# Where four blocks of modulation weights run: amid the attention, or among and behind the projections

## The chip, the core and the metric

The kernel runs on one NeuronCore of a Trainium2 chip. The metric is the time of the whole program on the device in microseconds (us). The five engines are named as in the profile: PE (matmul; PEld is its weight load), DVE (vector), ACT (scalar), POOL (GpSimd) and SP (which here only issues transfers). All of them run their own instruction lists in order and meet at semaphores.

## What is computed

One step of a one-layer decoder for a prompt group (512 tokens) and a sample group (8 sequences of 4 tokens) that share the weights. Both are modulated by six vectors that come from a conditioning vector c by one matrix of 1024 x 6144, in 12 blocks of 512 columns:

```python
def layer(x, c, ...):
    m = silu(c) @ w_ada + b_ada          # 6 modulation vectors of 1024
    sh1, sc1, g1, sh2, sc2, g2 = split(m, 6)
    h = rmsnorm(x) * (1 + sc1) + sh1
    u = h @ w_in                         # q, k, v of three branches, gates, z, xBC, dt
    o_nsa = nsa(u)                       # compressed, selected and window attention
    y_ssm = mamba2(u)                    # conv, scan, gate
    x = x + g1 * (concat(norm(o_nsa), norm(y_ssm)) @ w_out)
    h2 = rmsnorm(x) * (1 + sc2) + sh2
    return x + g2 * moe(h2)              # 16 experts, 2 per token
```

For the sample group the keys of 2048 earlier tokens are read from paged caches. The compressed branch takes pooled rows of a cache (a weighted sum over 32 rows), the selected branch gathers 16 blocks that the compressed scores choose.

## The kernel before

The program has three stages. In the **projections** the product with `w_in` runs in the pieces C, z, q and B, with three matmuls for each product (a weight split into `wh` and `wl`, the input into `hH` and `hL`, tile `acc`). Between the pieces stand the steps of the prompt's scan (p, c0 to c3, e). The string `ORDER` sets the sequence; `f1` in it calls `fill`, which runs one filler, and the table `BETWEEN` puts further fillers inside the pieces. A filler is either a pooling batch (`pool_batch`: two gathers of 1 MB of the compressed cache, issued by POOL, then 64 matmuls with `gcmp` and `PW`) or a modulation block (`ada_block`: two loads of 1 MB, `wada`, issued by SP, then 64 matmuls with the transposed conditioning vector `scT`, 8 with the bias `bada`, and one copy by ACT into `mods`). `in_turn` chains the matmuls of successive fillers so that PE takes them in that order. All these weights, gathers and the `w_in` pieces share a pool of 7 slots of 1 MB (`SLOT`, `load_w`), which is handed round in program order: a load starts when the reader of the slot's former content is through.

In the **attention**, `attend(t, b)` works through the prompt's branches (`s<-KT,QT`, softmax on DVE and ACT, transposes `pt<-ident,psb`, then `ot`), while the sample's chain (`sel_first`, `sel_second`: gathers `gsel`, tiles `sm`, `smo`; and the sample's scan, `sbm`, `xcS`, `s2k`) is a row of dependent steps. Then come the **output projection** and the **experts**.

Blocks 0 to 3 of the modulation are computed at the start. Blocks 4 to 7 are fillers. Blocks 8 to 11 (`sc2` and `g2`) run, before the change, amid the attention, just ahead of `attend(3, 1, True)`: `late_rows` loads their 8 MB through two buffers named `wt`, and their matmuls are summed in the tile `pt`, of which there are two buffers that `attend` also uses for its transposes. `store_mods` writes `mods` to DRAM (`modd`), from where the output projection loads it in other layouts (`M`, `MS`, `h2T`).

Of the kernel before, what the change touches and what calls it, by code (L numbers as in the profile page):

```python
# [9 lines left out]
F32 = mybir.dt.float32  # L10
# [7 lines left out]
P = 128  # L18
# [4 lines left out]
TS = 4  # L23
NS = NB * TS
NE = 16
ORDER = "C p z c0 c1 q c2 f1 f1 c3 e B"
WB = 6
XAT = 4
LA = 4
# [21 lines left out]
def hybrid_step(ctx: ExitStack, tc: tile.TileContext, a, o):  # L51
    nc = tc.nc
    V, S, G, T, SP = nc.vector, nc.scalar, nc.gpsimd, nc.tensor, nc.sync
# [19 lines left out]
    def W(pl, shape, dt, tag, bufs=2):  # L73
        return pl.tile(list(shape), dt, name=nm(tag), tag=tag, bufs=bufs)
# [85 lines left out]
    w_ada = a["w_ada"][0].rearrange("(k p) n -> p k n", p=P)  # L160
# [18 lines left out]
    p1, close_p1 = pool("p1")  # L179
# [125 lines left out]
    def store_mods(n0, n1):  # L305
        for j in range(4):
            SP.dma_start(modd[:, n0:n1, j, :], mods[32 * j:32 * j + 9, n0:n1, :])
# [52 lines left out]
    def in_turn(f, *args):  # L360

        traced = nc.cur_bb.bb.instructions
        n0 = len(traced)
        r = f(*args)
        for i in traced[n0:]:
            if i.engine == mybir.EngineType.PE:
                if tail[0] is not None:
                    tc.add_manual_dep(i, tail[0].name, mybir.DependencyInfo(mybir.DependencyClass.NoSync,
                                                                            mybir.DependencyReason.DATA),
                                      reason="in_turn")  # L370
                tail[0] = i
        return r
# [157 lines left out]
    for kv, w8 in enumerate((wk8, wv8)):  # L530
# [4 lines left out]
    V.tensor_scalar_mul(Wp[:, 1], Wp[:, 0], wkp[:, 1:2])  # L535
    V.tensor_scalar_mul(Wp[:, 0], Wp[:, 0], wkp[:, 0:1])

    fillers = [(pool_batch if c == "p" else ada_block, int(i)) for c, i in
               (f for f in "p0 a4 p1 a5 p2 p3 a6 p4 p5 a7 p6 p7".split())]

    def fill(n=1):
        for _ in range(n):
# [4 lines left out]
                   B={1: (fill,), 3: (fill,), 5: (fill,)})  # L547
# [287 lines left out]
    for step in ORDER.split():  # L835
# [3 lines left out]
            ssd_chunk(int(step[1:]))  # L839
        else:  # L840
            steps[step]()
    store_mods(0, 4)
    close_ph()
    close_p1()
    close_psum()
# [520 lines left out]
    attend(2, 1, True)  # L1366
    sel_second(1, gt11, *first1)

    def late_rows(n):
        ts = []  # L1370
        for hf in range(2):
            t = W(p3, [P, 2, 4, 256], F32, "wt", 2).rearrange("p b i c -> p (b i c)").rearrange("p (k c) -> p k c", k=4)
            SP.dma_start(t, w_ada[:, 4 * hf:4 * hf + 4, n * 512:n * 512 + 512])
            ts.append(t)
        return lambda k: ts[k // 4][:, k % 4, :]

    for n in range(8, 12):
        in_turn(ada_block, n, late_rows(n), "pt")
    store_mods(4, 8)
    attend(3, 1, True)  # L1380

    k3 = kcv[:, 0:P].rearrange("p (g d) -> p g d", d=64)
# [805 lines left out]
```

## Time and profile before

| | us |
|---|---|
| program, median of 3 runs | 811.96 (806.91 to 815.54) |
| program, the profiled execution | 813.91 |
| its span | 812.2 |
| PE busy in the span | 714.6 (88%) |
| DVE busy | 492.2 (61%) |
| ACT busy | 348.4 (43%) |
| POOL busy | 142.1 (17%) |

The span is what the profiler saw of the engines; 1.7 us of the program's time lie outside of it. Times in the rows are us from the start of the span. A granted clock of 1.00 is TensorE at 2.4 GHz, and 0.5 would be 1.2 GHz. Busy times overlap between engines.

### The profile page before, as it was taken

What the parts mean: (1) busy time and instruction counts of PE and PEld (TensorE: products, weight loads), DVE (VectorE), ACT (ScalarE), POOL (GpSimd) and SP (SyncE); (2) the same over time, 40 slices, a digit from 0 to 9 for tenths busy, and PEclk for the clock granted to TensorE, in tenths of its full rate; (3) what the DMA queues carried; (4) which work ended last, traced back from release to release, by engine and by line L of the source; (5) the groups of instructions that cost most, each with busy time, mean ns of one, the idle gap of its engine ahead of it and who ended that gap; (6) DMA issues with size and microseconds to landing.
All of it is one profiled execution on the core that took longest, in us unless ns stands there. A gap on an engine that the chain in (4) does not pass through costs nothing. (4 is left out here: it accounts for less than half of the span.)

```text
span 812.2 us, 14470 instructions
## 1 busy us (share of the span) xinstructions
PE 714.6 (88%) x5484; PEld 519.0 (64%) x5484; DVE 492.2 (61%) x1302; ACT 348.4 (43%) x799; POOL 142.1 (17%) x165
## 2 busy tenths in 40 slices
PE   4999999899897999659989788899948999999993
PEld 3677877777674766437456365678835676667662
DVE  7443783526529774354324644758996797887773
ACT  3324444425234435311133344623433575677671
POOL 3012021231313101012000100003131222224221
PEclk9999999899996979865599899999859999999997
DMA  8954885054474661482635310748858899998311
GB/s 287 391 128 154 297 307 205 2 189 151 180 272 164 233 232 46 163 311 104 196 122 206 112 45 1 235 156 285 323 175 339 247 311 338 316 335 281 85 22 26
DMA packets 67259, 161.86 MB, mean 199 GB/s; under 512 B 19171, under 2 KB 31404, under 8 KB 60788
## 3 DMA queue, kind: packets, MB, share of 16 engines
q1 hardware_dynamic: 56964, 115.54, 40.8%
q0 software_dynamic: 10224, 45.37, 16.6%
q8 instruction: 44, 0.72, 0.4%
q14 instruction: 27, 0.22, 0.1%
HBM read 153.48 MB, written 20.74 MB: 215 GB/s over the span
## 5 line engine op out<-in xcount | busy, mean ns | idle before, releaser
L892 ACT ACTIVATE psb<-s,amx 128x128 f32<-128x128 f32 (+3 forms) x64 | 33.2, 523 | 53.4 <-DVE amx L888 26.2
L95 PE MATMUL acc<-wh,hH 128*128 128x512 f32 (+1 forms) x128 | 49.2, 385 | 0.5 <-PE acc L95 0.5
L95 PE MATMUL acc<-wl,hH 128*128 128x512 f32 (+1 forms) x128 | 47.6, 372 | 0.0
L95 PE MATMUL acc<-wh,hL 128*128 128x512 f32 (+1 forms) x128 | 47.4, 370 | 0.0
L95 PE MATMUL acc<-gu,XF 128*128 128x512 f32 x88 | 46.5, 611 | 0.0
L95 PE MATMUL acc<-wh,XH 128*128 128x512 f32 x68 | 44.5, 655 | 0.4 <-ACT XH L1954 0.4
L344 DVE TENSOR_TENSOR wl<-dn,wh 128x512 fp32r<-128x512 f32 x52 | 34.1, 686 | 8.3 <-ACT wh L343 8.2
L895 PE MATMUL pt<-ident,psb 128*128 128x128 f32 x160 | 30.3, 298 | 10.0 <-ACT psb L892 9.4
L105 ACT COPY kt<-sm 128x512 f32<-128x512 f32 x33 | 19.0, 586 | 41.6 <-PE sm L1036 31.1
L344 DVE TENSOR_TENSOR wl<-gu,wh 128x512 fp32r<-128x512 f32 x44 | 29.6, 688 | 10.4 <-ACT wh L343 8.8
L343 ACT CAST wh<-dn 128x512 fp32r<-128x512 f32 x52 | 30.8, 619 | 10.7 <-PE acc L95 8.8
L2003 POOL DMA_INDIRECT out_y_prompt<-yo,gi x13 | 21.2, 1629 | 76.7 <-DVE gi L1923 16.8
L95 PE MATMUL acc<-wh,HH 128*128 128x512 f32 x68 | 32.3, 478 | 2.1 <-ACT HH L1986 2.1
L1071 POOL DMA_INDIRECT gsel<-in_cache_sel,idx x16 | 16.0, 1001 | 100.2 <-PE smo L95 71.2
L343 ACT CAST wh<-gu 128x512 fp32r<-128x512 f32 x44 | 26.2, 619 | 16.7 <-PE acc L95 10.3
L895 PEld LDWEIGHTS pt<-ident,psb 128*128 128x128 f32 x160 | 18.9, 150 | 19.0 <-ACT psb L892 14.8
L1724 POOL TENSOR_TENSOR h<-x,M 128x512 f32<-128x512 f32 x4 | 8.8, 2214 | 122.6 <-DVE x L1699 94.2
L95 PE MATMUL s<-KT,QT 64*128 64x384 f32 (+3 forms) x128 | 29.3, 521 | 0.8 <-ACT KT L863 0.8
L888 DVE TENSOR_REDUCE amx<-s 128x1 f32<-128x384 f32 (+1 forms) x32 | 18.5, 619 | 18.8 <-PE s L95 18.8
L95 PE MATMUL acc<-wl,XH 128*128 128x512 f32 x68 | 29.1, 427 | 0.8 <-DVE wl L344 0.8
L95 PE MATMUL ps<-wada,scT 128*32 128x128 f32 x512 | 27.8, 282 | 1.5 <-DVE modT L433 1.0
L95 PE MATMUL acc<-wl,HH 128*128 128x512 f32 x68 | 29.0, 427 | 0.0
(783 smaller groups left out, 1922.1 us busy)
## 6 DMA issues: line engine op xcount, KB each, us to landing
wada<-in_w_ada SPq DMA_DIRECT2D x16, 1024.0 KB
dn<-in_w_down SPq DMA_DIRECT2D x12, 1024.0 KB
gu<-in_w_gate SPq DMA_DIRECT2D x21, 512.0 KB
gu<-in_w_up SPq DMA_DIRECT2D x21, 512.0 KB
wt<-in_w_ada SPq DMA_DIRECT2D x8, 1024.0 KB
gux<-in_w_gate SPq DMA_DIRECT2D x11, 512.0 KB
gux<-in_w_up SPq DMA_DIRECT2D x11, 512.0 KB
wt<-in_cache_win SPq DMA_DIRECT2D x4, 1024.0 KB
```

Source lines behind the costliest of these rows:

```text
L95: T.matmul(out, lhsT, rhs, start=start, stop=stop)
L105: S.copy(out, in_)
L343: S.copy(wh[:, 0:n], w)
L344: (eng or V).tensor_sub(wl[:, 0:n], w, wh[:, 0:n].bitcast(F32))
L888: V.tensor_reduce(mx[:, g:g + 1], s2[:, g, 0:n], axis=AX.X, op=OP.max, negate=True)
L892: S.activation(pb[:, 0:n], s2[:, g, 0:n], AF.Exp, bias=mx[:, g:g + 1], accum_out=sm[:, h:h + 1])
L895: T.transpose(pt[:, c * P:(c + 1) * P], pb[:, c * P:(c + 1) * P], ident)
L1071: G.indirect_dma_start(out=t.rearrange("p r c -> p (r c)"), out_offset=None, in_=sel_rows, in_offset=bass.IndirectOffsetOnAxis(ap=idx[:, 2 ...
L1724: G.tensor_mul(h2s[t][:, 0:512], x1[:, t, 0:512], M[:, 2, 0:512])
L2003: G.indirect_dma_start(out=y_p, out_offset=bass.IndirectOffsetOnAxis(ap=gi, axis=0), in_=yo, in_offset=None, bounds_check=511, oob_is_err= ...
```

## The change

The fillers become sixteen: blocks 8 to 11 are among them, through the 7 slots and with the PSUM tile of the projections. Twelve fillers still run up to the end of piece B, as before; among them are now six blocks and six pooling batches, where there were four blocks and eight batches. Four more `f1` behind B run the rest: block 10, pooling batch 6, block 11 and pooling batch 7. `late_rows` and its loop leave the attention, and `store_mods` writes all eight blocks at once before it.

```diff
--- before.py
+++ after.py
@@ -23,7 +23,7 @@
 TS = 4
 NS = NB * TS
 NE = 16
-ORDER = "C p z c0 c1 q c2 f1 f1 c3 e B"
+ORDER = "C p z c0 c1 q c2 f1 f1 c3 e B f1 f1 f1 f1"
 WB = 6
 XAT = 4
 LA = 4
@@ -535,8 +535,8 @@
     V.tensor_scalar_mul(Wp[:, 1], Wp[:, 0], wkp[:, 1:2])
     V.tensor_scalar_mul(Wp[:, 0], Wp[:, 0], wkp[:, 0:1])
 
-    fillers = [(pool_batch if c == "p" else ada_block, int(i)) for c, i in
-               (f for f in "p0 a4 p1 a5 p2 p3 a6 p4 p5 a7 p6 p7".split())]
+    fillers = [(pool_batch if c[0] == "p" else ada_block, int(c[1:])) for c in
+               (f for f in "p0 a4 p1 a5 p2 a6 p3 a7 p4 a8 p5 a9 a10 p6 a11 p7".split())]
 
     def fill(n=1):
         for _ in range(n):
@@ -839,7 +839,7 @@
             ssd_chunk(int(step[1:]))
         else:
             steps[step]()
-    store_mods(0, 4)
+    store_mods(0, 8)
     close_ph()
     close_p1()
     close_psum()
@@ -1366,17 +1366,6 @@
     attend(2, 1, True)
     sel_second(1, gt11, *first1)
 
-    def late_rows(n):
-        ts = []
-        for hf in range(2):
-            t = W(p3, [P, 2, 4, 256], F32, "wt", 2).rearrange("p b i c -> p (b i c)").rearrange("p (k c) -> p k c", k=4)
-            SP.dma_start(t, w_ada[:, 4 * hf:4 * hf + 4, n * 512:n * 512 + 512])
-            ts.append(t)
-        return lambda k: ts[k // 4][:, k % 4, :]
-
-    for n in range(8, 12):
-        in_turn(ada_block, n, late_rows(n), "pt")
-    store_mods(4, 8)
     attend(3, 1, True)
 
     k3 = kcv[:, 0:P].rearrange("p (g d) -> p g d", d=64)
```

The first place is PE's list where piece B ends and the attention begins (`x4k,Wp` is the prompt's pooling, `ident,qa` the first transposes of the attention, `ident,wino` those of the window keys). Before:

```order
L95 MATMUL acc_2383<-wh_2631,hH 128x512
L95 MATMUL acc_2383<-wl_2632,hH 128x512
L95 MATMUL acc_2383<-wh_2631,hL 128x512
L95 MATMUL ps_2671<-x4k_848,Wp_842 16x128 x8
L973 MATMUL pt_2812<-ident,qa 128x128 x4
L973 MATMUL pt_2818<-ident,qa 128x128 x4
L973 MATMUL pt_2824<-ident,qa 128x128 x4
L973 MATMUL pt_2830<-ident,qa 128x128 x4
L862 MATMUL pt_2851<-ident,wino 128x128 x4
L95 MATMUL s_3223<-KT,QT 128x128 x2
```

After, the same stretch:

```order
L95 MATMUL acc_2387<-wh_2639,hL 128x512
L95 MATMUL ps_2679<-x4k_848,Wp_842 16x128 x5
L95 MATMUL ps_2731<-wada_2727,scT 32x128 x15
L95 MATMUL ps_2731<-bada,e_138 32x128 x4
L95 MATMUL ps_2773<-gcmp_2769,PW_839 32x128
...
L95 MATMUL ps_2773<-gcmp_2771,PW_839 32x128
L95 MATMUL ps_2811<-wada_2809,scT 32x128 x16
L95 MATMUL ps_2811<-wada_2807,scT 32x128 x16
L95 MATMUL ps_2811<-bada,e_138 32x128 x4
L95 MATMUL ps_2853<-gcmp_2849,PW_839 32x128
...
L95 MATMUL ps_2853<-gcmp_2851,PW_839 32x128
L973 MATMUL pt_2980<-ident,qa 128x128 x4
```

Between the last `acc` and the transposes there now stand two modulation blocks and two pooling batches.

The second place is PE's list in the sample's scan (`sm<-sbm`, `sm<-s2k`). Before, a late block's matmuls (`pt<-wt,scT`) stand between its steps:

```order
L95 MATMUL pt_4439<-wt_4437,scT 32x128 x12
L95 MATMUL sm_3824<-s2k_3718,dcS_3809 32x64 x8
L95 MATMUL sm_3840<-sbm_3837,s2k_3789 128x512
L95 MATMUL pt_4439<-wt_4437,scT 32x128 x4
L95 MATMUL pt_4439<-wt_4435,scT 32x128 x9
L95 MATMUL sm_3844<-sbm_3837,s2k_3789 128x512
L95 MATMUL pt_4439<-wt_4435,scT 32x128 x5
L95 MATMUL sm_3848<-sbm_3837,s2k_3789 128x512
L95 MATMUL pt_4439<-wt_4435,scT 32x128 x2
L95 MATMUL pt_4439<-bada,e_138 32x128 x4
L95 MATMUL sm_3852<-sbm_3837,s2k_3789 128x512
L1036 MATMUL sm_3882<-ident,gsel_3213 128x128 x4
```

After, the prompt's attention does (`s`, `ot`, and the transposes into `pt`):

```order
L95 MATMUL sm_3992<-s2k_3886,dcS_3977 32x64 x8
L95 MATMUL sm_4008<-sbm_4005,s2k_3957 128x512
L95 MATMUL ot_4760<-selo,ptsb_4848 128x64 x2
L95 MATMUL ot_4760<-selo,ptsb_4857 128x64 x2
L895 MATMUL pt_4879<-ident,psb_4877 128x128 x3
L895 MATMUL pt_4890<-ident,psb_4888 128x128 x3
L95 MATMUL s_4899<-KT,QT 128x384 x2
L95 MATMUL sm_4012<-sbm_4005,s2k_3957 128x512
L95 LDWEIGHTS identb
L95 MATMUL s_4899<-negm,identb 128x128
L95 LDWEIGHTS identb
L95 MATMUL s_4899<-negm,identb 128x128
```

The blocks have gone from the list there, and `attend(2, 1)` and `attend(3, 1)` have moved up to where they were; the last 53 rows of PE ahead of the output projection are now of the sample's second choice alone.

The third place is SP's list at the end of the projections, with buffer numbers. Before:

```order
L169 DMA wB_380_2376<-in_w_in 128x4x512
L169 DMA wB_381_2378<-in_w_in 128x4x512
L169 DMA wada_391_2417<-in_w_ada 128x4x512
L169 DMA wada_392_2419<-in_w_ada 128x4x512
L729 DMA out_ssm_prompt<-ts_376_2352 64x4x64 x2
L307 DMA modd_280<-mods_279 9x4x128 x4
L948 DMA out_cmp_sample<-us_115_825 32x256
L763 DMA out_cmp_prompt<-x4k_119_848 128x4x256
L1130 DMA wt_447_2857<-in_cache_win 128x2x1024
L1130 DMA wt_448_2859<-in_cache_win 128x2x1024
```

After:

```order
L169 DMA wada_391_2421<-in_w_ada 128x4x512
L169 DMA wada_392_2423<-in_w_ada 128x4x512
L169 DMA wada_405_2581<-in_w_ada 128x4x512
L169 DMA wada_406_2583<-in_w_ada 128x4x512
L169 DMA wada_421_2727<-in_w_ada 128x4x512
L729 DMA out_ssm_prompt<-ts_376_2356 64x4x64 x2
L169 DMA wada_422_2729<-in_w_ada 128x4x512
L169 DMA wada_427_2807<-in_w_ada 128x4x512
L169 DMA wada_428_2809<-in_w_ada 128x4x512
L948 DMA out_cmp_sample<-us_115_825 32x256
L763 DMA out_cmp_prompt<-x4k_119_848 128x4x256
L764 DMA out_sel_prompt<-selo_849 128x4x256
```

Six more loads of 1 MB from `w_ada` stand behind those of piece B, ahead of the outputs, of the stores of `modd` and of the window cache (`wt<-in_cache_win`, the row after next). The eight loads of `wt` from `w_ada` that followed later are gone.

## Rows read from the trace of the kernel before

**Rows 1.** Page, part 2: granted clock in 40 equal slices of the span.
```profile
PEclk9999999899996979865599899999859999999997
```

**Rows 2.** Windows by stage: stretch, length, busy time of each engine, granted clock, DMA share, GB/s.
```profile
85.00:243.90 158.90, 151.68 (x1586) 122.21 (x1581) 81.36 (x205) 61.51 (x158) 37.31 (x35) 0.96 0.55 198
243.90:268.20 24.30, 18.36 (x105) 13.33 (x104) 20.97 (x75) 11.39 (x40) 7.89 (x8) 0.65 0.56 196
268.20:318.30 50.10, 47.73 (x385) 32.88 (x384) 34.64 (x102) 25.54 (x83) 2.48 (x4) 0.90 0.43 160
318.30:510.40 192.10, 158.35 (x1381) 106.56 (x1379) 83.97 (x215) 60.45 (x155) 16.63 (x28) 0.83 0.39 138
```

**Rows 3.** Windows inside the attention, as above.
```profile
318.30:457.00 138.70, 111.89 (x1047) 75.14 (x1045) 57.56 (x149) 37.19 (x88) 16.63 (x28) 0.77 0.47 168
328.20:344.70 16.50, 12.28 (x124) 7.72 (x124) 6.29 (x22) 6.20 (x15) 0.00 (x0) 0.79 0.30 118
345.00:420.00 75.00, 61.44 (x560) 40.03 (x562) 30.39 (x82) 13.69 (x33) 9.38 (x9) 0.66 0.57 197
450.00:510.40 60.40, 50.25 (x375) 34.51 (x375) 31.68 (x81) 26.56 (x77) 3.17 (x15) 0.94 0.15 53
```

**Rows 4.** Windows of the attention, tile scT (block matmuls) and tile bada (bias) alone.
```profile
318.30:510.40 192.10, 17.15 (x256) 11.84 (x256) 0.00 (x0) 0.83 0.39 138
318.30:510.40 192.10, 3.00 (x32) 0.95 (x32) 0.83 0.39 138
```

**Rows 5.** Waits of PE in the attention: total, times, longest.
```profile
PE pt L95 <- DMA wt<-in_w_ada: 3.7, 2, 3.0
PE sm L1028 <- ACT sn L1026: 9.9, 3, 4.0
```

**Rows 6.** Timeline of PE, last late block: start, busy, instruction, idle before and releaser.
```profile
413.79 3.44 PE L95 MATMUL pt<-wt,scT 128*32 128x128 f32 x64 [3.00 <-DMA wt<-in_w_ada]
418.55 0.66 PE L895 MATMUL pt<-ident,psb 128*128 128x128 f32 x4
```

**Rows 7.** Timeline of SP, the last two late loads.
```profile
402.32 3.60 SPq L1373 DMA_DIRECT2D wt<-in_w_ada  x2
```

**Rows 8.** Timeline of PE, end of the projections and start of the attention.
```profile
218.26 1.95 PE L95 MATMUL ps<-wada,scT 128*32 128x128 f32 x64 [0.42 <-DVE ts L685]
220.50 0.50 PE L95 MATMUL acc<-wh,hH 128*128 128x512 f32 x1
235.12 1.96 PE L95 MATMUL ps<-gcmp,PW 128*32 128x128 f32 x64
237.00 0.50 PE L95 MATMUL acc<-wh,hH 128*128 128x512 f32 x1
239.95 1.08 PE L95 MATMUL ps<-wB,hsT 128*32 128x128 f32 x32
243.90 2.03 PE L95 MATMUL ps<-x4k,Wp 128*16 128x128 f32 x16
245.86 1.99 PE L973 MATMUL pt<-ident,qa 128*128 128x128 f32 x12
```

**Rows 9.** Timelines of POOL and PE: the last gather of a group and its first reader.
```profile
323.00 0.94 POOL L1071 DMA_INDIRECT gsel<-in_cache_sel,idx  x1 [0.30 <-issue]
328.22 1.48 PE L1036 MATMUL sm<-ident,gsel 128*128 128x128 f32 x8 [3.73 <-DMA gsel<-in_cache_sel,idx]
```

**Rows 10.** Window amid the projections, as in Rows 2.
```profile
225.00:235.00 10.00, 9.91 (x126) 7.85 (x124) 2.35 (x6) 4.48 (x8) 2.82 (x3) 1.00 1.01 398
```

**Rows 11.** Timeline of PE, prompt and sample pieces interleaved.
```profile
306.63 0.82 PE L895 MATMUL pt<-ident,psb 128*128 128x128 f32 x6
307.38 0.92 PE L95 MATMUL s<-KT,QT 64*128 64x384 f32 x4
308.35 1.04 PE L1036 MATMUL sm<-ident,gsel 128*128 128x128 f32 x8
```

**Rows 12.** Timeline of DVE, start of the output projection.
```profile
519.45 1.23 DVE L1520 SCALAR_TENSOR_TENSOR M<-M,h 128x1024 f32<-128x1024 f32 x1 [1.39 <-DMA h<-in_g_norm]
```

## The prediction, on record before the changed kernel ran

> **What bounds the kernel now.** I read the view by stage first. In the projections PE is busy for 151.68 of 158.90 us, so that work added there costs its own time and little else [rows 2]. The attention from 318.3 to 510.4 us is the loosest long stretch: 158.35 busy in 192.10, at a mean granted clock of 0.83 [rows 2], and the middle slices of the clock row, down to 5 and 6, are this stretch and the hand-over ahead of it [rows 1]. Cut finer, it has two parts. Up to 457 us the sample's chain runs with the late blocks between its steps: 111.89 busy in 138.70 at a clock of 0.77; its core, 345 to 420, has the clock at 0.66 [rows 3]. After that the prompt's attention is almost alone: 50.25 busy in 60.40 [rows 3]. The reader is to see two rows of dependent work one after the other, each of which leaves PE idle between its steps, though neither needs the other.
>
> Why they stand in a row shows at the last block. Its matmuls wait 3.00 us for their weights, which SP asked for between 402.32 and 405.9 [rows 6, 7]; only at 418.55 comes the next prompt transpose into `pt` [rows 6]. `pt` has two buffers, handed round in program order, and the blocks come ahead of `attend(3, 1)` in it. So everything of the prompt from `attend(3, 1)` on is held until the last block has its weights.
>
> Beside it, the same two kinds of work do run together before that: from 268.2 to 318.3 us prompt pieces and sample pieces alternate, and PE is busy for 47.73 of 50.10 at a clock of 0.90 [rows 2]. The timeline there shows a prompt transpose, a score piece and a sample transpose with no idle time noted ahead of any of them [rows 11].
>
> **Step 1, the attention without the blocks.** The blocks' own matmuls are 17.15 + 3.00 = 20.15 us of PE [rows 4]. Without them 158.35 − 20.15 = 138.2 us of PE work are left in the stretch. What matters is how tightly it packs. Bounds: as the prompt's attention alone packed, 50.25/60.40 = 0.832, which gives 138.2/0.832 = 166 us; or as the mixed stretch did, 47.73/50.10 = 0.953, which gives 145 us. I take 0.953, since the order now puts `attend(2, 1)` and `attend(3, 1)` between the steps of the sample's scan, which is what the mixed stretch looks like. To that comes an end that is the sample's alone: the last 53 rows of PE are its second choice with nothing of the prompt left. The nearest row for such a chain is 328.2 to 344.7 us, with 16.50 − 12.28 = 4.2 us idle [rows 3]; I add 6 with a wait at the end for the sum of the sample's outputs, which the output projection reads. 145 + 6 = 151, against 192.1: **−41 us**. At the loose bound it is 166 − 192 = −26.
>
> A third bound comes from the chain. It took 138.7 us to 457; of these 20.15 were the blocks and 3.7 PE's waits for their weights [rows 3 to 5], so the chain without them is about 115 us. The forecast of 151 doesn't ask it to be faster than that.
>
> **Step 2, the hand-over behind piece B.** Two blocks and two pooling batches now stand between the last `acc` and the first transposes of the attention, and PE takes them in order. A block cost 220.50 − 218.26 = 2.24 us, a batch 237.00 − 235.12 = 1.88 [rows 8]; two of each make 8.2. Beside this, the stretch 243.9 to 268.2 has 24.30 − 18.36 = 5.9 us of idle PE [rows 2], in which DVE (20.97 of 24.30) prepares keys and queries. If all of that went into the fillers' time, the cost would be +2.7 us or a little less: the lower bound.
>
> The upper bound comes from the slots. Going through the loads in program order, the first half of block 10 gets the slot of the second half of `wB`, which PE reads until 239.95 + 1.08 = 241.0 [rows 8]. The second gather of batch 7 gets the slot of that first half, so it starts when block 10 is through. From the last late load's issue to its first use was at most 413.79 − 405.9 = 7.9 us [rows 6, 7], and from the last gather's issue to its first reader 328.22 − 323.00 = 5.2 us [rows 9]. So block 10 could be done as late as 241.0 + 7.9 + 2.2 = 251.1; the gather lands at 256.3, the batch ends at 258.2, and the transposes, at 245.86 before [rows 8], begin some 13 us late; with 3 us more if the clock falls in these waits, as it did to 0.65 in this stretch [rows 2], +16. What queues behind are all of PE's attention, and on SP, which is in order too, the outputs and the loads of the window cache. POOL's queue holds two `memset`s and copies of the selected rows between the gathers. I take **+11**, nearer to the upper end, because the loads crowd: amid the projections the transfers already ran at a DMA share of 1.01 and 398 GB/s [rows 10], and the four loads and four gathers of these fillers, 8 MB, are 20 us at that rate, of which only those can start before 240 whose slots are free by then.
>
> That POOL issues the gathers and SP the loads gives no second path: the Trainium skill, "DMA: Bandwidth & Descriptors", section "Issuing engines are not separate DMA queues", says that transfers started by different engines end on the same 16 DMA engines and interleave there. This speaks against the change. If the two streams had paths of their own, step 2 would be near its lower end, +3; with the shared path it is near +16, and the 1.01 share in rows 10, with loads of both kinds under way, agrees with the page.
>
> **Step 3, inside the projections.** Two blocks in place of two batches: 2 × (2.24 − 1.88) = **+0.7 us**; each has the same 2 MB, and the slots are the same.
>
> **Step 4, the output projection: 0.** Its `modd` is written long before; the row that bounded its start was DVE's wait of 1.39 us for a load [rows 12]. The last quarter of `w_out` and one expert weight now load there too, since the slots come round later: 2 MB, 5 us at 398 GB/s, at worst if nothing covers them; against that, the scaling of the prompt's attention is off the end. I keep −3 to +6 for the range. The removal of eight loads from SP's list amid the attention gains nothing by itself; the transfers only move. ACT's copies, one a block, move too and cost nothing, since ACT is busy for 61.51 of 158.90 there [rows 2].
>
> **Sum.** −41 + 11 + 0.7 + 0 = −29. On the profiled execution: 813.9 − 29.3 = 784.6 (span 812.2 to about 783, and 1.7 outside). That execution is 1.95 us above the median, so against the median: **783 us**.
>
> **Rivals.**
>
> *The gain is half.* The two chains mix no better than the prompt's attention alone, and the hand-over costs its upper bound: −26 + 16 + 0.7 = −9 us, 803. For it: the waits for ACT in the chain (9.9 us in 3 waits, [rows 5]) are latencies that more work hides only if it is ready just then. Against it: the mixed stretch. Chance 0.18.
>
> *The clock comes back.* The mean granted clock of 0.83 rises to the 0.90 of the mixed stretch as the idle gaps close [rows 2]: 138.2 × 0.83/0.90 = 127.5 us of work, /0.953 = 134, + 6 = 140, which is −52; the sum is −40, 772 us. For it: 345 to 420, the slowest part, has the late blocks' waits in it. The Trainium skill, "TensorE: Matmul & The Clock Gate" (its glossary), prices throttled time at its length times the part of the clock that is missing; by that, a mean of 0.83 over 192 us would give back at most 33 us, of which my rows-based rival takes 11. Against it: the chain stays a chain, and the hand-over adds waits of its own. Chance 0.10.
>
> *Slower: prompt pieces hold the sample's chain back.* PE takes its list in order, so a sample step that is ready waits behind a prompt piece that is ahead of it and not ready. In the new order there are 37 places where a sample piece follows a prompt piece between the chain's first gather and the attention's end. The price of one is up to a transpose and a score piece, 0.82 + 0.92 = 1.7 us of work [rows 11], plus the wait for softmax between them. With the chain at 115, the whole is slower by over 1% from a stretch of about 188 us, so from (188 − 115)/37 = 2.0 us a place. At 2.5 us it would be 115 + 93 = 208, which is +16, and with step 2 +27: 839 us. Against it: the mixed stretch has such places and no idle time at them [rows 11]. Chance 0.08.
>
> **How the numbers follow.** The forecast has 0.64, the three rivals 0.18, 0.10 and 0.08. About 1%, 8 us, is what a measurement of this kernel can tell from no change: below 804 is faster. The forecast and the clock rival are faster, of the half gain some 0.07 is: 0.81. The rest of it is 0.11, within 1%; 0.08 slower. The range takes the bounds of steps 1, 2 and 4 around 783 and reaches toward the rivals of the same sign: 765 to 807. It leaves out the slower case and a part of the clock's.
>
> **What the profile of the changed kernel would show.** Step 1: a stretch from the first selected gather to the output projection of some 150 us, with PE busy at 0.9 or more and no window like 345 to 420 at 0.66. Step 2: PE waiting for DMA at `gcmp` or `wada` behind the last `acc`, and the `ident,qa` transposes some 11 us later behind it than the 2 us of before. Step 4: the output projection as long as before from its first `ident,zy`. The prediction fails if PE's waits in the sample's last rows are long (the sample's chain, not PE, then sets the end), if the gathers at the hand-over take longer than those in the attention, or if `w_out` comes late.

## The result, and the profile after

The changed kernel takes 775.28 us (median of 4 runs, 774.46 to 778.43), beside 811.96 of the kernel before (three runs, 806.91 to 815.54). Runs over 1.5% above the fastest of the same kernel, here the fourth of the kernel before at 823.56, belong to a slower state and are left out of all times and ratios. The ratio is 0.9561, 95% interval 0.9490 to 0.9633: faster by 36 us, where 29 were forecast. The profiled execution took 775.52 with a span of 773.8.

Six landmarks cut both spans at the same work: the first `x4k,Wp` (end of the projections), the first `ident,qa` (end of the hand-over), the first `smo<-gsel,kt` (from there the stretch that the prediction called the attention), the first `ident,zy` (output projection), the first `wout,catS` in it, the first `ident,h2S` behind it, and the end. Their places are PE's in the timelines of both kernels.

| stretch | before | after | difference | forecast |
|---|---|---|---|---|
| start to `x4k,Wp` | 243.9 | 246.4 | +2.5 | +0.7 (step 3) |
| to `ident,qa` | 2.0 | 13.1 | +11.1 | +11 (step 2) |
| to `smo<-gsel,kt` | 72.4 | 70.0 | −2.4 | in step 2 |
| to `ident,zy` | 192.2 | 149.6 | −42.7 | −41 (step 1) |
| to `wout,catS` | 35.1 | 29.6 | −5.5 | 0 (step 4) |
| to `ident,h2S` | 24.2 | 21.9 | −2.3 | 0 (step 4) |
| to the end | 242.3 | 243.3 | +0.9 | 0 |

The view by stage of the changed kernel (stretch, length, busy time of PE, PEld, DVE, ACT and POOL, granted clock, DMA share, GB/s) answers to [rows 2, 3]:

```profile
85.00:246.40 161.40, 153.58 (x1599) 122.93 (x1599) 81.03 (x205) 61.51 (x158) 32.68 (x30) 0.95 0.59 208
246.40:259.45 13.05, 11.74 (x289) 9.11 (x289) 6.10 (x27) 2.33 (x10) 6.61 (x9) 1.00 0.92 321
259.45:329.45 70.00, 63.66 (x471) 45.07 (x468) 50.07 (x148) 35.59 (x115) 8.34 (x8) 0.83 0.56 213
329.45:479.00 149.55, 139.07 (x1093) 96.90 (x1091) 83.70 (x233) 62.33 (x161) 15.76 (x28) 0.83 0.28 102
407.00:479.00 72.00, 66.53 (x508) 45.19 (x507) 39.87 (x115) 34.51 (x87) 3.87 (x16) 0.81 0.28 94
```

The attention is 149.55 us with PE busy for 139.07: 0.93, where it was 0.82. The mean clock is 0.83 in both, so the gain didn't come from the clock. From 407 us on it is 0.81.

The same stretch cut at 464.46, where PE's last prompt piece ends and the sample's steps are alone:

```profile
329.45:464.46 135.01, 129.28 (x985) 90.34 (x987) 72.51 (x183) 52.25 (x137) 15.76 (x28) 0.84 0.30 109
464.46:479.01 14.55, 9.80 (x114) 6.57 (x113) 11.19 (x50) 10.08 (x25) 0.00 (x0) 0.77 0.09 33
```

While both run, PE is idle for 5.7 us of 135.0; in the end that is the sample's alone, for 4.75 of 14.55.

The end of that stretch shows what changed. Before, PE's timeline (start, busy, instruction) has a score piece of `attend(3, 1)` ahead of all the blocks, whose first matmul is at 363.72; the transposes that follow from it come only at 418.55, behind the last block [rows 6]. Then come the last steps of the sample's second choice and, much later, the output projection:

```profile
322.70 1.13 PE L95 MATMUL s<-KT,QT 64*128 64x512 f32 x4
455.24 3.65 PE L95 MATMUL smo<-gsel,kt 128*32 128x128 f32 x64
510.51 1.04 PE L1533 MATMUL ps<-ident,zy 128*128 128x128 f32 x8
```

After:

```profile
456.53 1.13 PE L95 MATMUL s<-KT,QT 64*128 64x512 f32 x4
473.31 0.40 PE L1028 MATMUL sm<-ident,sn 128*32 128x128 f32 x1 [3.65 <-ACT sn L1026]
475.34 3.39 PE L95 MATMUL smo<-gsel,kt 128*32 128x128 f32 x64
479.01 1.09 PE L1522 MATMUL ps<-ident,zy 128*128 128x128 f32 x8
```

Before, the sample's chain ended at 458.9 and 51.6 us of the prompt's attention were left. After, the last score piece of the prompt is at 456.53, the chain ends at 478.7, and the output projection follows 0.3 us later. PE's longest waits there are the chain's own (total, times, longest):

```profile
PE sm L1028 <- ACT sn L1026: 6.1, 2, 3.6
PE sm L1036 <- DVE kt L103: 1.3, 2, 0.8
```

The waits of [rows 5] for `wt` are gone, and the wait for `sn` is 6.1 instead of 9.9.

The hand-over, PE's timeline behind the last `acc` (block 10's matmuls, between those of `x4k,Wp` from 246.39 on, are left out):

```profile
246.38 0.28 PE L95 MATMUL ps<-x4k,Wp 128*16 128x128 f32 x1
249.97 0.42 PE L95 MATMUL ps<-bada,e 12*32 12x128 f32 x8
250.32 2.00 PE L95 MATMUL ps<-gcmp,PW 128*32 128x128 f32 x47
252.64 0.73 PE L95 MATMUL ps<-gcmp,PW 128*32 128x128 f32 x17 [0.31 <-issue]
253.12 2.24 PE L95 MATMUL ps<-wada,scT 128*32 128x128 f32 x56
255.65 0.42 PE L95 MATMUL ps<-wada,scT 128*32 128x128 f32 x5 [0.29 <-issue]
256.37 0.41 PE L95 MATMUL ps<-wada,scT 128*32 128x128 f32 x3 [0.30 <-issue]
257.98 1.54 PE L95 MATMUL ps<-gcmp,PW 128*32 128x128 f32 x47 [0.18 <-issue]
259.45 0.77 PE L973 MATMUL pt<-ident,qa 128*128 128x128 f32 x5
```

It is as long as forecast, but PE doesn't wait for a transfer in this execution: in the view by stage it is busy for 11.74 of 13.05 us at a clock of 1.00, and the gaps are of 0.2 to 0.3 us with "issue" as releaser, which means that the profile shows nothing that PE waited for. Another execution of the same kernel (e8, below) has a hand-over of 11.1 us. There block 11 has no gaps, and the last batch does wait for its gather:

```profile
250.84 1.93 PE L95 MATMUL ps<-wada,scT 128*32 128x128 f32 x64
254.35 1.95 PE L95 MATMUL ps<-gcmp,PW 128*32 128x128 f32 x62 [0.90 <-DMA gcmp<-in_cache_cmp,idx]
```

### The profile page after: what moved, and what is told of

Its sections match the earlier page's. It is cut to its first block, busy times and chain, and to the rows that moved or that the text cites. A ratio compares the mean times of both kernels' runs of the same rounds, so it can differ in the third digit from the quotient of the medians.

```text
span 773.8 us, 14453 instructions
## 1 busy us (share of the span) xinstructions
PE 704.8 (91%) x5484; PEld 519.0 (67%) x5484; DVE 489.2 (63%) x1302; ACT 346.8 (45%) x799; POOL 138.6 (18%) x165
## 5 line engine op out<-in xcount | busy, mean ns | idle before, releaser
L892 ACT ACTIVATE psb<-s,amx 128x128 f32<-128x128 f32 (+3 forms) x64 | 33.2, 524 | 51.7 <-DVE amx L888 25.4
L95 PE MATMUL ps<-wada,scT 128*32 128x128 f32 x768 | 40.2, 304 | 3.2 <-DVE modT L433 2.1
L95 PEld LDWEIGHTS ps<-wada,scT 128*32 128x32 f32 x768 | 31.7, 122 | 9.5 <-issue 4.5
L343 ACT CAST wh<-dn 128x512 fp32r<-128x512 f32 x52 | 30.8, 619 | 10.7 <-PE acc L95 8.8
L344 DVE TENSOR_TENSOR wl<-gu,wh 128x512 fp32r<-128x512 f32 x44 | 29.7, 689 | 8.5 <-ACT wh L343 7.7
L95 PE MATMUL s<-KT,QT 64*128 64x384 f32 (+3 forms) x128 | 33.4, 569 | 0.0
L343 ACT CAST wh<-gu 128x512 fp32r<-128x512 f32 x44 | 26.2, 620 | 13.1 <-PE acc L95 9.9
L1986 DVE TENSOR_TENSOR yo<-acc,M 128x512 f32<-128x512 f32 x34 | 23.2, 687 | 9.7 <-PE acc L95 8.8
L95 PEld LDWEIGHTS acc<-wh,hH 128*128 128x128 f32 x128 | 24.1, 188 | 7.2 <-issue 3.0
```

The source lines that it names most:

```text
L95: T.matmul(out, lhsT, rhs, start=start, stop=stop)
L343: S.copy(wh[:, 0:n], w)
L344: (eng or V).tensor_sub(wl[:, 0:n], w, wh[:, 0:n].bitcast(F32))
L892: S.activation(pb[:, 0:n], s2[:, g, 0:n], AF.Exp, bias=mx[:, g:g + 1], accum_out=sm[:, h:h + 1])
L1986: V.tensor_tensor(yo[:, cols], po, M5[:, cols], op=OP.mult)
```

## The experiments

All times are medians of the runs; ratios are to the kernel before in runs beside it, which for e6, e8 and e9 are only three (806.01 to 812.59). "Chain" is the time from the first `smo<-gsel,kt` to the end of the last one, "left" what stands between that and the first `ident,zy`; the two make the attention. "Out" is from there to `wout,catS`. All but the last two columns come from one profile each.

| kernel | hand-over | attention | chain | left | out | program | ratio (95%) |
|---|---|---|---|---|---|---|---|
| before | 2.0 | 192.2 | 140.6 | 51.6 | 35.1 | 811.96 | 1 |
| after | 13.1 | 149.6 | 149.3 | 0.3 | 29.6 | 775.28 | 0.9561 (0.9490 to 0.9633) |
| e1 blocks behind prompt | 2.0 | 165.6 | 144.0 | 21.6 | 29.2 | 780.36 | 0.9546 (0.9480 to 0.9611) |
| e2 blocks left out | 1.9 | 139.9 | 139.6 | 0.3 | 30.9 | 754.99 | 0.9214 (0.9127 to 0.9301) |
| e3 all inside | 1.9 | 150.0 | 149.7 | 0.3 | 29.6 | 785.87 | 0.9631 (0.9560 to 0.9703) |
| e4 blocks last | 14.4 | 152.2 | 151.9 | 0.3 | 29.4 | 777.45 | 0.9534 (0.9449 to 0.9619) |
| e6 scale late | 11.0 | 149.5 | 149.2 | 0.3 | 29.6 | 771.73 | 0.9521 (0.9448 to 0.9594) |
| e7 spread | 2.0 | 162.9 | 137.6 | 25.4 | 35.6 | 779.61, 789.31 | none |
| e8 after again | 11.1 | 141.5 | 141.2 | 0.3 | 29.7 | 769.36 | 0.9521 (0.9404 to 0.9639) |
| e9 two spread | 5.3 | 152.6 | 133.0 | 19.6 | 36.3 | 781.18 | 0.9651 (0.9542 to 0.9761) |
| e10 scale last | 13.0 | 149.5 | 149.2 | 0.3 | 31.8 | 774.41 | 0.9521 (0.9465 to 0.9578) |
| e11 one late | 9.5 | 142.1 | 141.6 | 0.5 | 29.8 | 764.52 | 0.9414 (0.9352 to 0.9476) |
| e12 no loads | 12.2 | 149.6 | 149.3 | 0.3 | 29.7 | 775.71 | 0.9535 (0.9475 to 0.9594) |
| e13 one ahead | 2.0 | 187.8 | 146.1 | 41.7 | 37.5 | 812.10 | 0.9989 (0.9939 to 1.0040) |

With two runs, e7 has no ratio.

**Where the blocks stand in the attention.** Theory: what queues behind the blocks in `pt` is held. Rival: the blocks' work and loads cost, wherever they stand.

```diff
 # e1, from the kernel before
-    for n in range(8, 12):
-        in_turn(ada_block, n, late_rows(n), "pt")
-    store_mods(4, 8)
     attend(3, 1, True)
...
     attend(3, 0)
+    for n in range(8, 12):
+        in_turn(ada_block, n, late_rows(n), "pt")
+    store_mods(4, 8)
```

> The kernel before with one edit: the loop over the four late blocks and its store stand behind the prompt's last attend instead of ahead of attend(3,1). Same loads through the same two buffers, same tile pt, and the projections and the hand-over as before. Theory (the blocks hold the prompt back through pt): the attention gains the 41 us of the prediction less what of the blocks' 20 us shows in the sample's last rows, and there is no hand-over to pay: 775 to 785 us. Rival (what costs is the blocks' own work and their 8 MB amid the attention, wherever they stand): within 8 us of the kernel before, 805 to 815.

780.36, as the theory has it. Same work and same loads at another place in the list: the attention is 26.6 us shorter. The ratio, 0.9546, is that of the changed kernel (0.9561): moving the blocks behind the prompt already gains as much as the whole change, although PE still waits for their loads there. Its windows, the last block and the output projection in PE's timeline:

```profile
321.60:450.00 128.40, 122.34 (x1031) 86.27 (x1031) 75.67 (x185) 53.90 (x141) 14.26 (x14) 0.91 0.36 132
450.00:487.20 37.20, 19.25 (x352) 14.39 (x350) 13.06 (x52) 11.48 (x28) 0.50 (x4) 0.73 0.73 259
482.96 3.64 PE L95 MATMUL pt<-wt,scT 128*32 128x128 f32 x64 [12.90 <-DMA wt<-in_w_ada]
487.11 1.07 PE L1534 MATMUL ps<-ident,zy 128*128 128x128 f32 x7
```

The part in which both chains run is tight (122.34 of 128.40, clock 0.91); then the end of the sample's chain and the blocks are what is left, with PE busy for 19.25 of 37.20 and a wait of 12.90 for the last weights.

This shows that the place of the blocks is what costs. It moves them in PE's list and in the turn of `pt` at once. That `pt` is what held the prompt is read from the trace of before, where the score piece at 322.70 went ahead of the blocks and the transposes that need `pt` did not; no run gave the blocks a tile of their own.

```diff
 # e2, from the kernel before
-    for n in range(8, 12):
-        in_turn(ada_block, n, late_rows(n), "pt")
+    S.copy(mods[:, 4:8, :], mods[:, 0:4, :])
     store_mods(4, 8)
```

> The kernel before without the four late blocks: their loads and matmuls are left out, and the modulation vectors that they give are filled with those of the first four, so the second half of the layer computes something else. Prices the blocks in their old and new place. Theory: 812 - 41 = 771, less 0 to 8 for the output projection, 763 to 771; so the price in the old place is some 45 and in the new place 775 less this, 5 to 12. Rival (the changed kernel gained something else as well, from the order of fillers): this one is slower than 775.

754.99, lower than either had it. The blocks cost some 60 us in the old place (815.55 beside it). The changed kernel didn't run beside it, so the price in the new place is known less well: 14 or 20 us by the times (e8's 769.36 or 775.28 less 754.99), 25 or 28 by the ratios (0.9521 or 0.9561 less 0.9214, of 812). The hand-over has 9.2 or 11.2 of it. The attention, 139.9, is 10 us shorter than in the changed kernel's first profile, with the same instructions; that is the clock, below.

```diff
 # e13, from the kernel before
-    for n in range(8, 12):
-        in_turn(ada_block, n, late_rows(n), "pt")
-    store_mods(4, 8)
     attend(3, 1, True)
+    for n in range(8, 12):
+        in_turn(ada_block, n, late_rows(n), "pt")
+    store_mods(4, 8)
```

> The kernel before with only attend(3,1) moved ahead of the late blocks; the compressed branch and attend(1,0) to attend(3,0) still stand behind them. A dose of the same: theory (what queues behind the blocks in pt is what is held): between the 192 us of before and the 165.6 of all ahead, 175 to 188 for the attention, program 795 to 808. Rival (any move of the blocks gives the gain): 165 to 170 and 780 to 787; (attend(3,1) is not held by pt): 191 to 193.

The attention is 187.8, just inside the theory's range, but the program, 812.10, is outside of it and no faster than the kernel before (0.9989). One piece ahead gives 4.4 us in the attention, where all of them ahead gave 26.6: the compressed branch and three more pieces still come behind the blocks, and the output projection is 2.4 us longer. The attention's window, the last step of the sample's chain and the last score piece of the prompt:

```profile
318.30:510.00 191.70, 163.22 (x1426) 110.70 (x1419) 85.55 (x223) 64.00 (x164) 16.18 (x28) 0.83 0.41 143
463.10 1.08 PE L95 MATMUL smo<-gsel,kt 128*32 128x128 f32 x32
498.93 1.13 PE L95 MATMUL s<-KT,QT 64*128 64x512 f32 x4
```

The chain ends at 464.2 and the prompt runs on to 506: 41.7 us are left instead of 51.6, while the chain itself is 5.5 us longer.

```diff
 # e7, from the kernel before: one block behind each of
 # attend(3, 1), the compressed branch, attend(1, 0), attend(2, 0)
     attend(3, 1, True)
+    in_turn(ada_block, 8, late_rows(8), "pt")
...
+    in_turn(ada_block, 9, late_rows(9), "pt")
     attend(1, 0)
+    in_turn(ada_block, 10, late_rows(10), "pt")
     attend(2, 0)
+    in_turn(ada_block, 11, late_rows(11), "pt")
+    store_mods(4, 8)
     attend(3, 0)
```

> The kernel before with its four late blocks spread over the attention instead of in one row: one each behind attend(3,1), behind the compressed branch, behind attend(1,0) and behind attend(2,0), same two buffers and tile pt. Each block's loads then have a prompt piece's time to land. Theory (not the work but waits for loads in one row hold PE): no hand-over, attention 150 plus the blocks' 9 to 12 us, against 165.6 with all four behind the prompt: 765 to 777. Rival (a block amid the attention costs its 20 us as before, at the low clock): 780 to 790.

The theory missed: 779.61 and 789.31, at the edge of the rival's range and in it. PE doesn't wait for weights here, so waits for loads aren't all that blocks amid the attention cost: with them in between the prompt is the last to end again, 25.4 us are left behind the chain, and the output projection takes 35.6.

**The hand-over.** The prediction put most of its price on loads and a gather that wait for slots.

```diff
 # e12, from the changed kernel
+    kept = []
+    def ada_kept(n):
+        if n == 9:
+            kept.append(load_w(w_ada, n * 512, 512, "wada"))
+        return ada_block(n, kept[0])
+    fillers = [(ada_kept if f is ada_block and i > 8 else f, i) for f, i in fillers]
```

> The changed kernel where blocks 10 and 11 are computed with block 9's weights: 4 MB of loads are left out, so their part of the modulation is wrong; PE's instructions are the same. Tells transfers from PE work in the hand-over. Theory of transfers (slots and the shared path set it): from the first x4k to the first ident,qa 13.1 falls to 9 us or less. Rival (PE's own work sets it): 12 to 13 us.

12.2 us: the rival. With 4 MB less the DMA share in the hand-over falls from 0.92 to 0.73, and ahead of it, from 232 to 246 us, from 1.02 to 0.59, but PE's time stays: the hand-overs of the changed kernel's own list are 13.1, 13.0, 11.1 and 11.0 us (after, e10, e8, e6), and 12.2 lies among them. The two windows, at the changed kernel's times, and block 11 in PE's timeline, whose weights have long been there:

```profile
232.00:246.00 14.00, 14.00 (x157) 10.75 (x157) 1.84 (x4) 4.42 (x15) 2.36 (x4) 1.00 0.59 225
246.40:259.50 13.10, 11.66 (x284) 9.31 (x277) 6.10 (x27) 3.15 (x13) 4.74 (x7) 1.00 0.73 256
251.54 1.58 PE L95 MATMUL ps<-wada,scT 128*32 128x128 f32 x49
253.33 0.45 PE L95 MATMUL ps<-wada,scT 128*32 128x128 f32 x5 [0.20 <-issue]
254.08 0.44 PE L95 MATMUL ps<-wada,scT 128*32 128x128 f32 x6 [0.31 <-issue]
```

The block still takes from 251.54 to 255.5, in pieces with gaps of 0.2 to 0.3 us and the releaser "issue". So the pauses aren't its weights; what they are stays open. They are in after, e10 and e12. In e8 and e6 there are none; PE waits there 0.90 and 0.82 us for the last gather instead. In the paused executions the gather has landed by the time PE comes to it.

```diff
 # e4, from the changed kernel
-... a6 p3 a7 p4 a8 p5 a9 a10 p6 a11 p7
+... p3 a6 p4 p5 a7 p6 p7 a8 a9 a10 a11
 # e9, from the changed kernel: only p6 p7 behind piece B
-... a8 p5 a9 a10 p6 a11 p7
+... a8 p5 a9 p6 p7
     attend(3, 1, True)
+    in_turn(ada_block, 10, late_rows(10), "pt")
...
+    in_turn(ada_block, 11, late_rows(11), "pt")
+    store_mods(6, 8)
     attend(1, 0)
```

> The changed kernel with the fillers in the old order up to piece B (four blocks, eight batches) and blocks 8 to 11 all behind it. No gather stands behind B any more; work on PE there is 4 x 2.24 = 9 us instead of 8.2. Theory of the prediction (a gather that waits for a slot sets the hand-over): it shrinks by 3 to 5 us and the projections lose 0.7: 769 to 773. Rival (transfers under the same load, or PE's own work, set it): 774 to 780.

> The changed kernel with only pooling batches 6 and 7 behind piece B; blocks 10 and 11 run in the attention through the two buffers of the window cache, behind attend(3,1) and behind the compressed branch. Theory: the hand-over falls from 13 to 6 or 7 us and the attention pays 5 us or less: 768 to 775. Rival (DVE's and POOL's preparation sets the hand-over, and the blocks cost 5 us each in the attention): 776 to 784.

Both programs came out in the rival's range, but not both for its reason. Four blocks and no gather make the hand-over 14.4, two batches alone 5.3. Over the 2.0 of before that is 3.1 us a block and 1.7 us a batch. The batches are PE's own time (1.88 by [rows 8]), with little hidden, so that the theory was right there, and DVE's and POOL's preparation doesn't set the hand-over. The blocks are 2.24 us of PE each, and e4 has a wait of 2.11 us ahead of the last one. The profile puts it down to a DVE step that the block doesn't read. SP had issued the block's second load at 245.14, 8.8 us ahead of its first matmul at 253.96, so the load is the likelier cause; that isn't shown. In e9 the saving is lost behind the chain: two blocks amid the attention leave 19.6 us of prompt there, and the output projection takes 36.3.

```diff
 # e3, from the changed kernel
-ORDER = "C p z c0 c1 q c2 f1 f1 c3 e B f1 f1 f1 f1"
+ORDER = "C p z c0 f1 c1 f1 q c2 f1 f1 c3 f1 e f1 B"
```

> The changed kernel with the four fillers from behind piece B moved ahead of it, one behind each of c0, c1, c3 and e, so that all sixteen run among the projections and the scan chunks; their list is the same. Theory: the 11 us of the hand-over go, and 0 to 8 us of them come back as work in the projections: 765 to 773. Rival (the slots, not the place, are what the hand-over pays: loads that start no earlier make PE wait inside instead): 774 to 782.

785.87, worse than both had it. The hand-over's 11 us go, but the projections end at 265.2 instead of 246.4. From 200 to 230 us the changed kernel, then e3, the longest wait in PE's timeline and what ACT did ahead of it:

```profile
200.00:230.00 30.00, 27.37 (x335) 21.69 (x331) 18.59 (x50) 9.18 (x23) 10.36 (x8) 0.97 0.61 215
```

```profile
200.00:230.00 30.00, 23.43 (x243) 18.85 (x245) 17.67 (x45) 6.34 (x16) 6.61 (x6) 0.61 0.40 141
214.00 0.79 PE L95 MATMUL ps<-xx 64*128 64x128 f32 x2 [4.14 <-ACT kvc L524]
212.64 1.14 ACT L343 CAST wh<-wB 128x512 fp32r<-128x512 f32 x2 [5.07 <-DMA wB<-in_w_in]
```

A scan chunk waits 4.14 us for ACT to copy a pooling batch out of its PSUM tile. ACT, in order, had first to split a weight of piece B, whose load kept it for 5.07 us; so the rival's mechanism, loads that make PE wait inside, is there, at a price above its range. Right behind the wait, from 214 to 230, the chunk's short steps run at a granted clock of 0.50 (1.2 GHz), with PE busy for 13.57 of 16.00; the changed kernel has 1.00 from 205 to 230. Over the projections (85 us to their end) PE's busy time rises by 15.7 us, of which the fillers' own work is 8.2, and its idle time by 3.1.

**The output projection.** It gained 7.8 us that the prediction had at 0: 5.5 in "out" and 2.3 in the stretch behind it. In every profile in which the prompt ends ahead of the sample (or of the blocks), "out" is 29.2 to 31.8; in the four in which the prompt ends last (before, e7, e9, e13) it is 35.1 to 37.5.

```diff
 # e6 and e10, from the changed kernel (e6: hb = 0 alone)
+    for hb in range(2):
+        V.scalar_tensor_tensor(ssa, osum[:, hb, 0:4], 0.0, ssa, op0=OP.mult, op1=OP.add)
     r = rstd(ssa, 512, "x")
```

> The changed kernel, where the scaling of the prompt's attention is made to wait for the sum of the sample's outputs (its sums of squares get 0 times that sum added). Tests where the 8 us came from that the output projection gained and that the prediction had at 0. Theory (the prompt's attention ends before the sample's, so its normalisation is off the end): the stretch from the first ident,zy to the first wout,catS goes back from 29.6 to about 35 us, program 780 to 784. Rival (the early loads of MS gave it): no change, 773 to 778.

> As e6_scale_late, but the scaling of the prompt's attention waits for both halves of the sample's sum; the first trial waited for one half only, which was ready long before the end. Theory (the prompt's attention is off the end in the changed kernel): from the first ident,zy to the first wout,catS 34 to 37 us instead of 29.6, program 5 to 8 us over the changed kernel. Rival (the early loads of MS): 29 to 31 us, no change.

e6 changed nothing, since the half that it waited for is ready early; it counts as one more run of the changed kernel. e10 did hold the scaling back. DVE's timeline of the changed kernel, then of e10:

```profile
468.21 0.16 DVE L137 TENSOR_SCALAR rstd_x<-ssa 128x4 f32<-128x4 f32 x1
472.04 1.67 DVE L1434 TENSOR_SCALAR qa<-qa,rsq_zx 128x512 f32<-128x512 f32 x4
```

```profile
466.28 0.15 DVE L1433 SCALAR_TENSOR_TENSOR ssa<-osum,ssa 128x4 f32<-128x4 f32 x1
477.75 0.16 DVE L1433 SCALAR_TENSOR_TENSOR ssa<-osum,ssa 128x4 f32<-128x4 f32 x1
482.83 1.67 DVE L1436 TENSOR_SCALAR qa<-qa,rsq_zx 128x512 f32<-128x512 f32 x4
492.92 1.23 DVE L1511 SCALAR_TENSOR_TENSOR M<-M,h 128x1024 f32<-128x1024 f32 x1 [1.85 <-DMA h<-in_g_norm]
```

The scaling of `qa` moves from 472.04 to 482.83, behind the second half of the sum at 477.75 (the first was there at 466.28), and "out" goes from 29.6 to 31.8: 2.2 of the 5.5 us. The program's time doesn't show it. DVE's wait for the load ahead of `M` [rows 12] is still there in e10, with 1.85 us.

PE's own waits tell more. Before, PE waits four times in "out", for 4.2 us in all; the two longest are

```profile
524.04 0.51 PE L95 MATMUL acc<-wl,catH 128*128 128x512 f32 x1 [1.87 <-DVE wl L344]
530.17 1.53 PE L1533 MATMUL ps<-ident,qa 128*128 128x128 f32 x8 [1.20 <-DVE qa L1445]
```

The first is for DVE's split of a weight, the second for the scaling of the prompt's attention; the others are for ACT, 0.67 and 0.48. The changed kernel has no wait of PE in "out", and e10 has one, 1.47 for `wl`. So 4.2 of the 5.5 us are these waits. That they come of the order of the ends, by which the prompt's scaling and the splits of the weights reach DVE and ACT when PE needs them, is read from the waits; e10 tested the scaling alone. In the stretch behind, PE is busy without a gap in both kernels, with 216 and 206 matmuls, so these 2.3 us are work at another place in its list; the stretch is 24.2 in e1 too, whose prompt ends ahead, and the last stretch of the changed kernel is 0.9 longer.

**The clock, and one block late.**

> The changed kernel once more, beside the others on one chip, and a second profile of it. Theory that the clock in the last third of the attention differs from one execution to the next: attention between 140 and 152 us with the same waits, and a program time of 770 to 779. Rival (0.81 there belongs to this order): attention 149 to 150 and a clock of 0.83 again.

The same kernel gives 141.5 us for the attention in another execution. Its two windows, and below them those of e2:

```profile
326.40:467.90 141.50, 130.80 (x1094) 92.32 (x1092) 84.21 (x233) 62.33 (x161) 15.76 (x28) 0.89 0.30 108
404.00:467.90 63.90, 58.43 (x508) 41.13 (x508) 39.66 (x114) 34.50 (x87) 3.87 (x16) 0.94 0.32 106
```

```profile
321.80:461.70 139.90, 129.10 (x1093) 90.78 (x1091) 85.46 (x233) 62.43 (x161) 16.20 (x28) 0.90 0.30 109
400.00:461.70 61.70, 56.24 (x497) 39.80 (x496) 39.22 (x113) 34.13 (x86) 3.87 (x16) 0.94 0.33 109
```

From 404 us on the clock is 0.94 where the first profile has 0.81 from 407 on, and PE's busy time is 58.43 instead of 66.53: 8.1 us, the whole difference. The longest waits are the same to 0.1 us. PE's idle time in the attention is the same, 10.5 and 10.7 us, so that the length follows PE's busy time. The profiles fall into two groups: after, e3, e6, e10 and e12 have 149.5 to 150.0 us at 0.83, and e2, e8 and e11 have 139.9 to 142.1 at 0.89 or 0.90. e4, with 49 more matmuls in the stretch, has 152.2 at 0.88 and is in neither. What decides between them wasn't found.

```diff
 # e11, from the changed kernel
-... a9 a10 p6 a11 p7
+... a9 a10 p6 p7
...
     attend(3, 0)
+    in_turn(ada_block, 11, late_rows(11), "pt")
+    store_mods(7, 8)
```

> The changed kernel with one block, number 11, taken from behind piece B and put behind the prompt's last attend, through the two buffers of the window cache, so that both its halves can be loaded long before. Theory: the hand-over loses the block's 2.2 us and its 2 MB, 3 to 5 us; in the sample's last rows, where PE idles 4.75 of 15 us, it costs 0 to 3; output projection 29.6 as the sample still ends last: 764 to 772. Rival (it makes the end later by its own time): 771 to 778.

764.52, the fastest that computes everything, as the theory had it. The hand-over is 9.5; the block lies in the sample's last rows, and the chain is still what ends last. A window over most of its attention (which ends at 466.43) and the start of the output projection, the last step of the chain and the output projection:

```profile
329.00:475.00 146.00, 135.54 (x1145) 96.32 (x1144) 90.50 (x245) 65.36 (x167) 15.15 (x26) 0.89 0.38 136
462.31 3.64 PE L95 MATMUL smo<-gsel,kt 128*32 128x128 f32 x64
466.43 1.09 PE L1533 MATMUL ps<-ident,zy 128*128 128x128 f32 x8
```

Some of its lead over the changed kernel is the clock (0.89 from 329 to 475). Its four runs, 762.71 to 768.03, lie beside 765.27 to 778.43 in the twelve of the changed kernel, e6 and e8; its interval of the ratio to before ends just below the changed kernel's first one and overlaps that of e8. Beside it e10 and e12 took 774.41 and 775.71.

## Why the prediction was right, point by point

**Step 1, the attention: right, in size and term by term.** 149.6 us against 151. The work is 139.07 us of PE against 138.2; while both run PE is busy for 129.28 of 135.01, 0.96 against 0.953 (e1 has 122.34 of 128.40, 0.953); the end that is the sample's alone leaves PE idle for 4.75 us against 6. That the place of the blocks held the prompt back is shown by e1; that `pt` did it is read from the trace. e8 and e2 bear out that PE's work sets the length: with the clock at 0.89 and 0.90, PE's busy time and the attention shrink together and the idle time stays. The chain's own length was never measured alone. It took 133 to 152 us in every kernel, with blocks, with prompt pieces or with fewer blocks between its steps; the 51.6 us of prompt that stood behind it went in between and made it 8.7 us longer in place of the blocks' 20.15 and their waits. The third rival's condition is not met: (149.3 − 115)/37 places is 0.9 us each, below the 2.0 from which it would have decided; the 115 is a difference, so this is argued, not shown. One bound was read badly: the loose one, 50.25/60.40, is from a window that opens at 450, 9 us before the chain ends; from 458.9 on PE is busy for 44.76 of 51.60, 0.87, which makes that bound 159 us instead of 166.

**Step 2, the hand-over: right in size, in part by luck.** +11.1 against +11, but +9.1 in e8's execution. The prediction added up landing times. The first link of that chain failed: block 10 didn't wait for its loads, as PE ran it together with the pooling from 246.39 on, right behind the last `acc`; and e12, with 4 MB of loads less, gained nothing that stands out from the spread of the same list. So the choice of the upper end "because the loads crowd" was wrong. The last link, the gather that gets block 10's slot, is there, but it costs 0.90 and 0.82 us (e8, e6), and nothing in the executions with pauses. What the hand-over costs is PE's own work, 8.2 us by [rows 8], with nothing hidden; on top come that wait in e8 and e6, and in the first profile 2.9 us of slower work and pauses of open cause. That the sum met 11 in the profiled execution is luck. The sums of the bounds were a little off: the transposes would be 12.3 us late, not 13 (258.2 − 245.86), and the lower bound is 2.3, not 2.7 (8.24 − 5.94). The lower bound also let the 5.9 us of idle PE take up the fillers. That idle time lies behind the first transposes, since DVE prepares from them, and work ahead of them didn't fill it: only 2.4 us came back, in the stretch after. The Trainium skill, "DMA: Bandwidth & Descriptors", section "Issuing engines are not separate DMA queues", still agrees with the trace, whose DMA share in the hand-over is 0.92 with transfers of SP and gathers of POOL under way; but PE's time hung on a transfer for 0.9 us at most, so the rule decided little here.

**Step 3: not to be told.** +2.5 against +0.7. Kernels with the same list up to there (before, e1, e2, e4, e7, e13) end the projections between 243.4 and 249.2 us.

**Step 4, the output projection: missed.** 0 was forecast, −7.8 came, outside its −3 to +6. The step that failed is the bound at its start: the prediction named DVE's wait for a load ahead of `M`, but that wait is still in e10 and PE's waits were others, 4.2 us for the prompt's scaling, its copy and the splits of weights. The later loads of `w_out` and of an expert weight cost nothing visible. That the prompt's scaling would be off the end stood in the text as a possible offset; holding it back costs 2.2 us by e10. These 7.8 are most of the distance between the forecast and the result.

**The clock rival** came out as a size, not as a case: 7 to 10 us in the attention, near the 11 that the prediction took from rows, but from one execution of the same kernel to another. The Trainium skill, "TensorE: Matmul & The Clock Gate", section "Terms", prices throttled time by the missing part of the clock; for the last third that is 72.0 × 0.19 = 13.7 against 63.9 × 0.06 = 3.8, an estimate of 9.9 us, and the trace gives 8.1.

## What to carry to other kernels

Where two dependent chains share an in-order engine, look at what is left of the one when the other ends; the place of a third kind of work matters by what it pushes behind that end, more than by its own time. Then add up the engine's work, how tightly it packed where both ran, and the end that one chain has alone: here that sum held. A small rotating buffer that two kinds of work share is an order between them: a block that waits for its weights in it holds all that comes later. Filler work fills an idle gap only if it stands in the gap; here, ahead of the instructions that the gap hangs on, it cost its full time and got 2.4 us back. And one profile is one execution: the same list had a hand-over of 13.1 and of 11.1 us, with another reason for the last 1 to 3 us in each.

## What the runs showed of the hardware that was not expected

- One kernel's attention took 149.6 and 141.5 us in two executions with the same waits; the granted clock of its last third was 0.81 in the one and 0.94 in the other, and eight of the nine profiles with this attention fall on one of these two sides.
- Behind a wait of 4.14 us in the scan (e3) the granted clock was 0.50 from 214 to 230 us, over short steps that kept PE busy for 13.57 of 16.00; four fillers of 8.2 us of work made the projections 18.8 us longer.
- A block with its weights in place took 4.0 us at the hand-over (e12, 251.54 to 255.5) instead of the 2.24 of [rows 8], in pieces with pauses for which the profile shows no cause, at a granted clock of 1.00; in another execution of the changed kernel (e8) it took 2.2 there, without pauses.
